# Strassen feed-forward stages rebuilt: units in sequence, the first product passed on in PSUM, row pairs for both halves, a fixed order on three engines

## The chip, the core and the metric

The kernel runs on one core of a Trainium2 chip. The metric is the device time of one execution in microseconds (us). The engines of the core are TensorE (PE: matmuls, and PEld: their weight loads), VectorE (DVE), ScalarE (ACT), GpSimd (POOL, here mostly an issuer of DMAs) and SyncE (SP, which issues the other DMAs). Each engine executes its own list of instructions in order and waits for semaphores of the others. [...]

## What is computed

One layer of a decoder trunk for 512 prompt tokens and 32 sample tokens (T = 544 together), width 1024:

```python
def swiglu(x, wg, wu, wd):
    return (jax.nn.silu(x @ wg) * (x @ wu)) @ wd

x = layer_norm(ALPHA * x + 0.5 * swiglu(x, ffn1_wg, ffn1_wu, ffn1_wd), ln1_g, ln1_b)
mix = ...            # RWKV-7 heads and a short convolution, both from x @ w_in, then @ w_out
x = layer_norm(ALPHA * x + mix, ln2_g, ln2_b)
x = layer_norm(ALPHA * x + 0.5 * swiglu(x, ffn2_wg, ffn2_wu, ffn2_wd), ln3_g, ln3_b)
```

The two feed-forward stages (1024 to 2816 to 1024) hold most of the matmuls. The change touches only them.

## The kernel before

**Layout.** Activations lie transposed: features on the 128 partitions, tokens along the row. A product in float32 precision is made of three matmuls: each operand is split into a high half (ScalarE, a copy that rounds to `F32R`) and a low half (VectorE, the operand minus its high half); the matmuls are high x high, high x low, low x high. So each weight tile costs one ScalarE and one VectorE pass beside its DMA. `hl` is a split weight tile, `hlb` a half-size one, `raw` the loaded one; `xhl` are the split inputs, `hhl` the split hidden rows, `z` the output sums.

**Strassen.** Both feed-forward products are done by a seven-product Strassen scheme (Winograd's form) on 2 x 2 blocks: tokens in two halves of 272 (`TB`), the inner dimension in two halves, the output rows in two. The 22 hidden row tiles come in chunks of 4, 4, 4, 4 and 6 (`CHUNKS`). Chunk 0's hidden rows are made by plain matmuls (`up`), the others by `pairs`. After each of chunks 0 to 3 `downs` multiplies its hidden rows by the down weights; chunk 4 goes to plain matmuls (`down`, `down_wide`).

- `pairs` works in units `u`: one unit makes gate or up of two hidden row tiles, so two units (even: gate, ended by Silu; odd: up, ended by a multiplication) make a row pair. A unit has seven products of 12 matmuls each, named by the weight tile: "a" twice, "x" twice, "y" twice, "b" once. `b1`, `b3`, `b4` are its PSUM banks (`mm` and `sm` in the profile, three and five of them). Bank `b1` goes on accumulating through a, y, x and b, and is copied out (to `cpb`) after each.
- `downs` has two groups of 14 products of 6 matmuls. Their inputs are seven combinations of the four hidden row tiles: `B11, B21, B22, NT1, NT2, T3, T4`.
- The weight combinations: "a" is a raw tile as loaded, "b" a half of the other raw tile, "x" that tile after an accumulating DMA by GpSimd has added the block A11 to it, "y" that tile after two VectorE additions. "y" and "a" free the raw tiles for the next loads (`feed`, `load`, five of them).

**What sets the order.** The program is recorded in the order of the generators, and a scheduler then places the instructions of every engine; it may pull a matmul of a later product ahead. Weight work is recorded by `plan`: an event for each part (`b`, `a`, `x`, `y`) at a lead, in products, ahead of the unit or group that needs it (`LEAD`, `LEAD_B`); `put` (L503) records the high and the low half together. Around them `held` keeps weight work behind the evictions of the product just recorded. Units are interleaved: in `pairs` (L562) the last two products of a unit (`tail`, L577) are recorded after the first two of the next.

**Hidden rows.** `put_h` (L366) makes the seven combinations. The halves of the inner dimension of the downs are row tiles (0, 1) and (2, 3) of a chunk: the first row pair is one half, the second pair the other. `NT2`, `T3` and `T4` mix both halves, so they wait for the second pair (the lines L383, L384, L387); `put_b22` splits both rows of `B22` at once.

**Names of lines used below.** L135/L136: high and low half of a weight tile. L143/L144: high and low half of other operands. L155 to L157: plain products. L521/L522: the additions for "y". L529/L535: the accumulating DMAs. L556 to L558: the three matmuls of a Strassen product. L599, L619, L627: VectorE's additions of a bank to `cpb` in a unit; L617, L623, L626: ScalarE's copies of `b1` in a unit. L646, L676: VectorE's additions in the downs; L662, L665: ScalarE's copies there.

Of the kernel before, what the change touches and what calls it, by code (L numbers as in the profile page):

```python
# [12 lines left out]
F32 = mybir.dt.float32  # L13
# [28 lines left out]
LEAD = dict(b=18, a=9, x=7, y=5)  # L42
LEAD_B = {0: 25, 1: 23}
# [18 lines left out]
def body(ctx: ExitStack, tc: tile.TileContext, xT, gu1, wd1, win, wo_c, wo_0, wo_1, gu2, wd2, wl, ln3, eye, lora, vec, cst,  # L62
# [260 lines left out]
    class Ffn:  # L323
        def __init__(self, z, gu, wd, ph, nf, late=1):
            self.z, self.gu, self.wd, self.na, self.nf, self.late = z, gu, wd, NA, nf, late
            self.ph, self.st, self.tst, self.w, self.nu = ph, ExitStack(), ExitStack(), {}, 0
            self.s1 = [cpb[:, 288 * h:288 * h + 288] for h in range(2)]
            self.lnr = cpb[:, 576:864]
# [37 lines left out]
        def put_h(self, j, r, parts):  # L366

            hb, (hk, sv) = self.hb, (x[:, r] for x in self.rows)
            lo, hi = slice(0, TB), slice(TB, T)

            def put(v, src):
                split(hb[:, v, 0, r], hb[:, v, 1, r], src)

            for part in parts:
                if j == 0 and part == "lo":
                    put(B11, hk[:, lo])
                elif j == 0:
                    DVE.tensor_tensor(hk[:, lo], hk[:, lo], hk[:, hi], op=OP.subtract)
                    put(NT1, hk[:, lo])
                elif part == "lo":  # L380
                    put(B21, sv[:, lo])
                elif part == "hi":
                    DVE.scalar_tensor_tensor(hk[:, lo], hk[:, lo], -1.0, sv[:, hi], op0=OP.mult, op1=OP.subtract)  # L383
                    DVE.tensor_tensor(hk[:, hi], sv[:, hi], hk[:, hi], op=OP.subtract)  # L384
                    put(slice(NT2, T3 + 1), hk.rearrange("p (v t) -> p v t", v=2))
                else:
                    DVE.scalar_tensor_tensor(sv[:, lo], hk[:, lo], -1.0, sv[:, lo], op0=OP.mult, op1=OP.subtract)  # L387
                    put(T4, sv[:, lo])

        def put_b22(self):  # L390
            split(self.hb[:, B22, 0], self.hb[:, B22, 1], self.rows[1][:, :, TB:])

        def up(self, m, h):
# [15 lines left out]
            if h:  # L409
                self.done.add(m)  # L410
                for m in [x for x in range(self.na) if x in self.done and (x < 2 or x - 2 in self.done)]:
                    if m not in self.made:
                        self.made.add(m)
# [1365 lines left out]
```

## Time and profile before

| | us |
|---|---|
| median of three runs | 1072.73 (1071.32 to 1073.76) |
| profiled execution, first to last instruction | 1069.3 |
| first feed-forward stage, Strassen part | 53.75 to 333.6 |
| second feed-forward stage, Strassen part | 742.6 to 1023.7 |
| one full chunk (4 units and the downs), repeated | 64.83 |

The profile is of one execution. Its page gives each engine's busy time and share of the span, then digits for 40 slices of the span, the DMA queues, the chain of work that ended last, and the costliest groups of instructions: line, engine, operation, output<-inputs, shape, xcount, then busy us, mean ns of one, and the idle time of the engine just before them with what ended it. A timeline row is start us, duration us, engine, line, operation, output<-inputs, shapes, count. A windows row gives busy time and count of instructions for PE, PEld, DVE, ACT and POOL in a stretch, then TensorE's granted clock, the DMA share and GB/s. Matmuls are pipelined, and the end of a row of TensorE is modelled.

### The profile page before, as it was taken

To read this page: it belongs to the slowest core of one execution; us is meant where nothing else is said; L and a number is where in the kernel's file an instruction comes from. 1 tells how busy PE (TensorE), PEld (TensorE's weight loads), DVE (VectorE), ACT (ScalarE), POOL (GpSimd) and SP (SyncE) were. 2 spreads that over 40 slices of the span, in tenths; PEclk is the share of its full clock that TensorE was granted. 3 is DMA by queue.
4 is the path that set the end of the run, shared out by engine and by line. 5 is a ranking of instruction groups with operands and counts; after the bars stand their busy time and mean duration, and the time that the engine had idled before them with its cause. 6 is when DMAs were issued, how large, how long until landed. Compare 5 with 4: busy or idle time off the path is not lost.

```text
span 1069.3 us, 22615 instructions
## 1 busy us (share of the span) xinstructions
PE 1050.8 (98%) x9178; PEld 1010.5 (95%) x9178; DVE 844.6 (79%) x1557; ACT 582.9 (55%) x1070; POOL 155.3 (15%) x273
## 2 busy tenths in 40 slices
PE   9999999999999999999999999999999999999997
PEld 8999999999999999899889988999999999999996
DVE  6797888979875777794578658888979888797657
ACT  5746465555553668654344435767555555655524
POOL 0121121211200032133101200001211212111000
PEclk9999999999999999999999999999999999999999
DMA  8558585676754223324145624334766948568512
GB/s 296 128 116 186 124 191 137 149 169 136 183 118 158 79 92 105 85 82 99 41 143 163 172 81 149 132 119 79 156 162 137 199 103 197 141 136 189 147 43 84
DMA packets 91528, 144.48 MB, mean 135 GB/s; under 512 B 34848, under 2 KB 52384, under 8 KB 91296
## 3 DMA queue, kind: packets, MB, share of 16 engines
q1 hardware_dynamic: 68144, 110.76, 33.7%
q0 software_dynamic: 22848, 31.72, 19.4%
q8 instruction: 72, 1.18, 0.4%
q10 hardware_dynamic: 432, 0.56, 0.2%
q14 instruction: 32, 0.26, 0.1%
HBM read 128.81 MB, written 9.75 MB: 130 GB/s over the span
## 4 chain that ended last, share of the span: by engine, by line
PE 77%; DVE 13%; ACT 6%; issue 2%; DMA 1%; POOL 0%; ACTq 0%; DVEq 0%; SPq 0%
PE mm L556 9%; PE mm L557 9%; PE mm L558 9%; PE mm L155 6%; PE sm L556 6%; PE sm L557 6%; PE sm L558 6%; PE mm L156 6%; PE mm L157 6%; DVE hhl L144 2%; DVE hl L136 2%; PE sm L444 1%; PE sm L1169 1%; ACT hl L135 1%; PE mm L787 1%
## 5 line engine op out<-in xcount | busy, mean ns | idle before, releaser
L136 DVE TENSOR_TENSOR hl<-raw,hl 128x1024 fp32r<-128x1024 f32 (+3 forms) x230 | 269.8, 1177 | 61.4 <-ACT hl L135 60.2
L135 ACT ACTIVATE hl<-raw 128x1024 fp32r<-128x1024 f32 (+3 forms) x230 | 232.8, 1020 | 67.3 <-DVE raw L522 43.5
L155 PE MATMUL mm<-xhl,hl 128*128 128x256 f32 (+1 forms) x704 | 208.9, 298 | 0.5 <-ACT xhl L143 0.5
L156 PE MATMUL mm<-xhl,hl 128*128 128x256 f32 (+1 forms) x704 | 203.0, 289 | 0.4 <-DVE xhl L144 0.4
L157 PE MATMUL mm<-xhl,hl 128*128 128x256 f32 (+1 forms) x704 | 202.0, 287 | 0.0
L155 PEld LDWEIGHTS mm<-xhl,hl 128*128 128x128 f32 x704 | 132.0, 188 | 6.7 <-issue 1.8
L156 PEld LDWEIGHTS mm<-xhl,hl 128*128 128x128 f32 x704 | 132.3, 188 | 2.4 <-DVE xhl L144 0.8
L157 PEld LDWEIGHTS mm<-xhl,hl 128*128 128x128 f32 x704 | 132.3, 188 | 0.3 <-issue 0.2
L558 PE MATMUL sm<-xhl,hl 128*128 128x272 f32 x432 | 125.2, 290 | 0.0
L557 PE MATMUL sm<-xhl,hl 128*128 128x272 f32 x432 | 124.4, 288 | 0.0
L556 PE MATMUL sm<-xhl,hl 128*128 128x272 f32 x432 | 124.1, 287 | 0.0
L556 PE MATMUL mm<-tv,hl 128*128 128x272 f32 x288 | 83.4, 290 | 0.3
L558 PE MATMUL mm<-tv,hl 128*128 128x272 f32 x288 | 83.4, 290 | 0.0
L557 PE MATMUL mm<-tv,hl 128*128 128x272 f32 x288 | 83.0, 288 | 0.0
L556 PEld LDWEIGHTS sm<-xhl,hl 128*128 128x128 f32 x432 | 81.3, 188 | 0.0
L557 PEld LDWEIGHTS sm<-xhl,hl 128*128 128x128 f32 x432 | 81.3, 188 | 0.0
L558 PEld LDWEIGHTS sm<-xhl,hl 128*128 128x128 f32 x432 | 81.3, 188 | 0.0
L535 POOL DMA_DIRECT2D raw<-in_wd x32 | 39.2, 1462 | 287.8 <-DVE hlb L144 225.2
L529 POOL DMA_DIRECT2D raw<-in_gu x36 | 43.3, 1203 | 203.0 <-DVE hlb L144 137.6
L557 PE MATMUL mm<-hhl,hl 128*128 128x272 f32 x192 | 56.0, 291 | 0.8 <-DVE hhl L144 0.2
L556 PE MATMUL mm<-hhl,hl 128*128 128x272 f32 x192 | 56.3, 299 | 0.3
L556 PEld LDWEIGHTS mm<-tv,hl 128*128 128x128 f32 x288 | 54.2, 188 | 1.9 <-ACT cpb L623 1.9
(421 smaller groups left out, 2713.5 us busy)
## 6 DMA issues: line engine op xcount, KB each, us to landing
raw<-in_gu SPq DMA_DIRECT2D x84, 512.0 KB, 4.4
raw<-in_gu POOLq DMA_DIRECT2D x36, 512.0 KB, 7.0
raw<-in_wd SPq DMA_DIRECT2D x32, 512.0 KB, 4.5
raw<-in_win SPq DMA_DIRECT2D x26, 512.0 KB, 3.6
raw<-in_wd POOLq DMA_DIRECT2D x32, 256.0 KB, 5.7
z<-sv POOLq DMA_DIRECT2D x16, 272.0 KB, 8.2
raw<-in_wo_c SPq DMA_DIRECT2D x8, 512.0 KB, 3.6
raw<-in_wd SPq DMA_DIRECT2D x8, 384.0 KB, 3.1
```

The source lines that it names most:

```text
L135: seen["hi"] = ACT.activation(hl[:, 0, a:b], raw[:, a:b], AF.Copy)
L136: seen["lo"] = DVE.tensor_tensor(hl[:, 1, a:b], raw[:, a:b], hl[:, 0, a:b].bitcast(F32), op=OP.subtract)
L144: return DVE.tensor_tensor(lo, x, hi.bitcast(F32), op=OP.subtract)
L155: PE.matmul(out, wh, src[:, 0, k, c0:c1], start=(start and i == 0), stop=False)
L156: PE.matmul(out, wh, src[:, 1, k, c0:c1], start=False, stop=False)
L157: seen["fill"] = PE.matmul(out, wl, src[:, 0, k, c0:c1], start=False, stop=(stop and i == n - 1))
L444: PE.matmul(o[i][h][:, :c1 - c0], block(hl, v, k), xhl[:, y, k, c0:c1], start=(k == 0 and j == 0), stop=(k == KD - 1 and j == 2), skip_gro ...
L529: POOL.dma_start(x.rearrange("p (s c) -> p s c", s=2), bass.AP(tensor=a11.tensor, offset=a11.offset, ap=[[2 * D, P], [P * 2 * D, 2], [1, 5 ...
L535: POOL.dma_start(four(x)[:, i], bass.AP(tensor=a11.tensor, offset=a11.offset, ap=[[DFF, P], [P * DFF, 2], [1, 256]]), accum_op=OP.add)
L556: PE.matmul(out, wh, src(0, i), start=(first and i == 0), stop=False, skip_group_check=True)
L557: PE.matmul(out, wh, src(1, i), start=False, stop=False, skip_group_check=True)
L558: PE.matmul(out, wl, src(0, i), start=False, stop=(i == n - 1), skip_group_check=True)
```

## The change

- *Units in sequence.* `pairs` runs the seven products of a unit one after the other, as a, x, y, y, x, a, b.
- *First product passed on in PSUM.* After the first "a" product ScalarE copies bank `b1` into bank `b4`, and the second "a" product goes on accumulating there. Before, `b4` began empty and VectorE added it to the copy of the first. The downs do the same with their first and last product on `b4` (`m1`, `m2`).
- *Row pairs feed both halves.* The host reorders the rows of the down weights, so that a row pair has one row in each half of the inner dimension. `put_h` makes all seven combinations of a pair when the pair is done; `B22` is split pair by pair.
- *Order of the downs.* Written as a list of names (`ORDER`, `FIRST`).
- *A fixed order on three engines.* Weight work (`PARTS`) and row work (`ROWS`) have places in half products, with places of their own for the high and the low half. `link` ties each ScalarE and each VectorE instruction of these stages to the one recorded before it, and `prod` does so for TensorE's products. Silu and multiplications of the even and odd units are done by halves of 272. `held` and `feed` go.

```diff
-LEAD = dict(b=18, a=9, x=7, y=5)
-LEAD_B = {0: 25, 1: 23}
+PARTS = {
+    "u0": dict(b=(-62, 7), a=(-31, 11), x=(-26, 7), c=(-17,), y=(-13, 3)),
...
+    "u3": dict(b=(-36, 10), a=(-12, 3), x=(-18, 11), c=(-6,), y=(-5, 1)),
...
+ROWS = {
+    (0, B11, 0): -17, (0, B11, 1): 1, (0, B21, 0): -3, (0, B21, 1): 13, (0, B22, 0): -25,
...
+LATE = -51
+ORDER = "m1 m1 m5 m5 u2 u2 m3 m3 u3 u3 m2 m2 u4 u4", "m1 m5 m1 m5 u2 u2 m3 m3 u3 u3 m2 m2 u4 u4"
+FIRST = "m1 m1 m5 m5 m2 u2 u2 m3 u3 m3 u3 m2 u4 u4", ORDER[1]
...
+        def link(self, q, e):
+            if self.fixed:
+                if self.prev[q] is not None:
+                    after(e, self.prev[q])
+                self.prev[q] = e
+            return e
...
+        def at(self, pos, f, *args):
+            self.ns += 1
+            heapq.heappush(self.steps, (pos, self.ns, f, args))
+
+        def run(self, pos):
+            while self.steps and self.steps[0][0] <= pos:
+                _, _, f, args = heapq.heappop(self.steps)
+                f(*args)
...
+        def put_h(self, p, *parts):
+
+            hk, sv = (self.rows[p][:, i] for i in range(2))
             lo, hi = slice(0, TB), slice(TB, T)
+            mix, n1 = cpb[:, 4 * TB:], cpb[:, 2 * TB:3 * TB]
+            ops = {NT1: (self.tt, n1, hk[:, lo], hk[:, hi]), T3: (self.tt, mix[:, hi], sv[:, hi], hk[:, hi]),
+                   NT2: (self.neg, mix[:, lo], hk[:, lo], mix[:, hi]), T4: (self.neg, hk[:, lo], mix[:, lo], sv[:, lo])}
...
+            now = 2 * self.t - 2
+            for part in parts:
+                if part in ops:
+                    f, *args = ops[part]
+                    self.at(now + ROWS[p, part, 2], f, *args, OP.subtract)
+            for part in parts:
+                if part in src:
+                    v = slice(NT2, T3 + 1) if part == NT2 else part
+                    dst = [self.hb[:, v, i, p] for i in range(2)]
+                    self.at(now + ROWS[p, part, 0], self.act, dst[0], src[part], AF.Copy)
+                    self.at(now + ROWS[p, part, 1], self.low, dst[1], src[part], dst[0])
...
+                    for part, pos in PARTS[kind].items():
+                        self.at(2 * t + pos[0], self.put, key, part)
+                        if part != "c":
+                            self.at(2 * t + pos[0] + pos[1], self.put_low, key, part)
...
         def prod(self, out, key, part, off, src, first, n=HK):
-            self.feed()
-            self.t += 1
+            self.run(2 * self.t)
...
+                if i == 0 and self.pe is not None:
+                    after(e, self.pe)
...
+            for u in range(m1 - m0):
                 j, i = divmod(u, 2)
-                s = self.rows[min(j, 1)]
+                a = 2 * TB * i
+                cp, s = cpb[:, a:a + 2 * TB], self.rows[j % 2]
+                b1, b4 = big()[:, :TB], sm()[:, :TB]
+                yield from prod(b1, u, "a", 0, xb(0, 0), True)
+                self.act(b4, b1, AF.Copy)
+                while self.add:
+                    self.tt(*self.add.popleft(), OP.add)
+                b3 = sm()[:, :TB]
+                yield from prod(b3, u, "x", HK, xb(0, TB), True)
+                self.act(cp[:, TB:], b3, AF.Copy)
+                yield from prod(b1, u, "y", HK, tb(0), False)
+                self.act(cp[:, 0:TB], b1, AF.Copy)
+                yield from prod(b3, u, "y", 0, xb(HK, TB), False)
+                self.tt(cp[:, 0:TB], cp[:, 0:TB], b3, OP.add)
...
+                yield from prod(b1, u, "x", 0, tb(1), False)
+                self.tt(cp[:, TB:], cp[:, TB:], b1, OP.add)
...
+                    if ci < LAST:
+                        self.put_h(j, B22)
+                yield from prod(b4, u, "a", HK, xb(HK, 0), False)
...
+                        self.put_h(j, B11, NT1, T3, NT2)
...
                 yield from prod(b1, u, "b", 0, tb(2), False)
...
+                        self.put_h(j, B21, T4)
...
+                def m1(q):
                     yield from prod(b1, q, "a", 0, B11, True)
-                    add(ds[q], b1[q])
+                    self.act(b4[q], b1[q], AF.Copy)
+
+                def m2(q):
+                    yield from prod(b4, q, "a", 1, B21, False)
+                    add(ds[q], b4[q])
+
+                def m5(q):
+                    yield from prod(b3, q, "x", 1, NT1, True)
+                    self.act(cp[q][:, 1], b3[q], AF.Copy, scale=-1.0)
+
+                def u2(q):
                     yield from prod(b1, q, "y", 1, NT2, False)
+                    self.act(cp[q][:, 0], b1[q], AF.Copy)
...
-        a["wd" + i] = tiles(g[f"ffn{i}_wd"][0]).reshape(KD, P, DFF)
+        order = list(first) + [b + k for b in (4, 8, 12) for k in (0, 2, 1, 3)] + list(range(16, MF))
+        a["wd" + i] = tiles(g[f"ffn{i}_wd"][0])[:, :, order].reshape(KD, P, DFF)
```

Of a place `(p, q)` in `PARTS`, p is where the high half of a part is recorded and q how much later the low half is, in half products from the start of the unit or group (a product of the downs is half as long as one of a unit); "c" are the additions for "y". In the downs `u3`, `m3` and `u4` follow the same pattern as `u2`: a product, then its eviction.

300 lines of the change are left out of this document (147 added, 153 removed).

## The prediction

> **What bounds the kernel now.** I read the page first: the shares of the engines and the chain that ended last, as shares by engine.
>
> ```profile
> span 1069.3 us, 22615 instructions
> PE 1050.8 (98%) x9178; PEld 1010.5 (95%) x9178; DVE 844.6 (79%) x1557; ACT 582.9 (55%) x1070; POOL 155.3 (15%) x273
> ...
> PEclk9999999999999999999999999999999999999999
> ...
> PE 77%; DVE 13%; ACT 6%; issue 2%; DMA 1%; POOL 0%; ACTq 0%; DVEq 0%; SPq 0%
> ```
>
> TensorE is the bound, at full clock, and the change removes no matmul: seven products for eight before and after. So it can only win the time in which TensorE's stream is held up, inside the two feed-forward stages. The sum is made as a difference against the profiled span of 1069.3 us; the median of the timed runs, 1072.73 us, is 3.4 us longer, which I leave as it is.
>
> How much is held up? A PE row lasts 0.29 us but the next starts 0.125 us later, so busy time hides short holds. I take starts instead. Next view: windows (us; busy time and count of instructions per engine).
>
> ```profile
> 146.20:179.50 33.30, 33.30 (x267) 33.30 (x267) 25.06 (x40) 19.58 (x34) 3.64 (x3) 1.00 0.70 166
> ...
> 112.00:176.80 64.80, 64.61 (x506) 63.54 (x505) 55.84 (x98) 35.73 (x62) 12.10 (x10) 1.00 0.69 155
> ...
> 53.75:111.95 58.20, 58.20 (x463) 57.80 (x462) 50.12 (x86) 31.18 (x54) 9.66 (x8) 1.00 0.65 146
> 306.40:333.50 27.10, 27.10 (x217) 27.00 (x216) 16.85 (x26) 15.38 (x27) 1.09 (x10) 1.00 0.45 130
> 742.70:801.95 59.25, 58.99 (x462) 58.00 (x461) 51.64 (x89) 32.60 (x57) 10.90 (x10) 1.00 0.69 152
> 996.30:1023.60 27.30, 27.30 (x217) 27.05 (x215) 17.64 (x27) 14.84 (x23) 0.00 (x0) 1.00 0.36 106
> ```
>
> The first row is an undisturbed stretch: 267 matmuls, one of them under way at its left edge, so 33.30 / 266 = 0.125 us from start to start. A full chunk repeats every 64.83 us, as the chain in order of time shows:
>
> ```profile
> 111.94 1.07 ACT hl L135
> ...
> 176.77 1.07 ACT hl L135
> ...
> 241.60 1.07 ACT hl L135
> ```
>
> It has 4 units x 7 products x 12 matmuls + 28 half-size products x 6 = 504 matmuls, or 504 x 0.125 = 63.1 us. So **1.7 us of each full chunk is hold-up**; there are three such chunks in each of the two stages: 10.2 us. The other four windows (first downs and part of chunk 1, and the last units, of each stage) give by count x 0.125, two of each count being under way at the edges: 0.6, 0.2, 1.75 and 0.4, together about 2.9. **About 13 us can be won at most**, 1.2%.
>
> [...]
>
> Where are the holds? Timeline, three places in chunk 1 (start us, us, engine, line; in brackets what the idle time waited for), then the chain that runs through the pairs-to-downs border.
>
> ```profile
> 114.59 0.40 ACT L626 ACTIVATE cpb<-mm 128x272 f32<-128x272 f32 x1 [0.76 <-PE mm L558]
> ...
> 115.04 0.19 PEld L556 LDWEIGHTS mm<-tv,hlb 128*128 128x128 f32 x1 [0.21 <-ACT cpb L626]
> 115.04 0.39 PE L556 MATMUL mm<-tv,hlb 128*128 128x272 f32 x1
> ...
> 115.27 0.29 PE L557 MATMUL mm<-tv,hlb 128*128 128x272 f32 x1
> ```
> ```profile
> 136.37 0.19 PEld L556 LDWEIGHTS mm<-hhl,hl 128*128 128x128 f32 x1 [0.25 <-ACT sv L662]
> ...
> 145.13 0.29 PE L558 MATMUL mm<-tv,hl 128*128 128x272 f32 x1
> ...
> 145.52 0.40 ACT L623 ACTIVATE cpb<-mm 128x272 f32<-128x272 f32 x1 [2.54 <-PE mm L558]
> ...
> 145.97 0.19 PEld L556 LDWEIGHTS mm<-tv,hl 128*128 128x128 f32 x1 [0.27 <-ACT cpb L623]
> ```
> ```profile
> 119.72 0.35 DVE z L646
> 120.06 0.35 DVE hhl L144
> 120.42 0.35 DVE hk L383
> 120.77 0.35 DVE hk L384
> 121.12 0.35 DVE sv L387
> 121.47 1.28 DVE hhl L144 x2
> 122.80 0.39 PE mm L557
> ```
>
> Two kinds. First, a bank that goes on accumulating must be copied out by ScalarE between two of its products (the first two fences); each such wait costs its own length plus about 0.1 us, since the first start after it is followed after 0.23 us (115.04 to 115.27) and not 0.125. Second, at the border the last row pair's sums and splits run one after the other on VectorE while the downs already need them.
>
> **The change part by part.**
>
> *Matmuls, weight loads, clock*: same number, same shapes: 0 us.
>
> *Border, pairs to downs.* With row pairs feeding both halves, the first pair's seven inputs can be made during units 2 and 3, and only the second pair's are left at the border. VectorE at the end of chunk 1, before (names: `hhl` the split inputs of the downs, `sv`/`hk` the rows, `z` the output):
>
> ```order
> L383 SCALAR_TENSOR_TENSOR hk<-hk,sv 128x272
> L384 TENSOR_TENSOR hk<-sv,hk 128x272
> L387 SCALAR_TENSOR_TENSOR sv<-hk,sv 128x272
> L144 TENSOR_TENSOR hhl<-sv,hhl 128x544
> L144 TENSOR_TENSOR hhl<-hk,hhl 128x2x272
> L144 TENSOR_TENSOR hhl<-sv,hhl 128x272
> L646 TENSOR_TENSOR z<-z,mm 128x272
> ```
>
> These stand after the first downs' additions; they are the chain above. The same engine and place now:
>
> ```order
> L400 TENSOR_TENSOR sv<-sv,sm 128x272
> L400 TENSOR_TENSOR cpb<-sv 128x272 x2
> L400 TENSOR_TENSOR hhl<-sv,hhl 128x272
> L403 SCALAR_TENSOR_TENSOR cpb<-sv,cpb 128x272
> L400 TENSOR_TENSOR hhl<-cpb,hhl 128x272
> L403 SCALAR_TENSOR_TENSOR sv<-mm,sv 128x272
> L403 SCALAR_TENSOR_TENSOR sv<-cpb,sv 128x272
> L400 TENSOR_TENSOR hhl<-sv,hhl 128x272
> L400 TENSOR_TENSOR hhl<-cpb,hhl 128x2x272
> L400 TENSOR_TENSOR hlb<-raw,hlb 128x512
> ```
>
> No addition to `z` and no first-pair work stands among them. I step them by 0.35 us for a 272-wide row (the chain's step) and 0.64 for a 544-wide one (1.28 for two). Zero is the end of the last unit's next-to-last product; the last product ends, and the downs begin, at 1.5. The first row starts at 0.1 and ends at 0.45, the two differences at 1.15, the low half of B11 at 1.5. The first downs need it for their second inner row, three matmuls and one in, at 1.5 + 0.5 = 2.0. NT1's low half ends at 2.2, needed at 3.5; NT2 and T3's at 3.9, needed at 5.0. All have half a microsecond or more, but for semaphores and the ScalarE half that stands ahead of each: a slip of a wait in B11 costs up to 0.2 us. I take 0.2 of the hold-up as staying here.
>
> *Evictions and the order of products.* In the downs the two copies are now four products apart ("u2 u2 m3 m3 u3 u3") where they were two, so the wait at 136.37 goes. In the units, every copy has exactly one other product (12 x 0.125 = 1.5 us) to hide under, four such windows in a unit (a to y and y to x on `b1`, x to y on `b3`, and x to b on `b1`, this one on VectorE). The 145.13 to 145.97 rows give the least a copy needs, from the last matmul's start to the next product's: 0.84 us. The window is 1.5 + 0.125 = 1.63, so **0.79 us of slack** for whatever ScalarE has in hand. The tightest place is after unit 1, where the first pair's splits now stand ahead of unit 2's first copy. ScalarE, before, at its first copy of unit 2 and what stands ahead:
>
> ```order
> L626 ACTIVATE cpb<-mm 128x272
> L135 ACTIVATE hl<-raw 128x1024
> L617 ACTIVATE cpb<-mm 128x272
> L135 ACTIVATE hl<-raw 128x1024
> L143 ACTIVATE hhl<-hk 128x272 x2
> L623 ACTIVATE cpb<-mm 128x272
> ```
>
> and now (`sm<-mm` is the new copy into the second bank):
>
> ```order
> L397 ACTIVATE hhl<-hk 128x272
> L397 ACTIVATE hl<-raw 128x1024
> L397 ACTIVATE hhl<-cpb 128x272
> L397 ACTIVATE hhl<-hk 128x272
> L397 ACTIVATE hhl<-cpb 128x2x272
> L397 ACTIVATE hlb<-raw 128x512
> L397 ACTIVATE hhl<-hk 128x272
> L397 ACTIVATE sm<-mm 128x272
> ```
>
> ```profile
> 124.02 1.05 ACT L135 ACTIVATE hl<-raw 128x1024 fp32r<-128x1024 f32 x1
> 124.97 0.39 ACT L662 ACTIVATE cpb<-mm 128x272 f32<-128x272 f32 x1
> 125.30 0.40 ACT L665 ACTIVATE cpb<-mm 128x272 f32<-128x272 f32 x1
> ```
>
> Seven rows now stand where four stood. By these starts a 1024-wide row steps by 0.95 and a 272-wide by 0.33; in proportion 0.55 for 544 or 512. From the end of unit 1's next-to-last product: product of the rows on VectorE done at 0.6, then 0.33 + 0.95 + 2 x 0.33 + 0.55 + 0.55 + 0.33 = 3.4, so the copy runs from 4.0 to 4.4; unit 2's third product may start at 1.5 + 1.5 + 1.5 = 4.5. It fits by 0.1, and loses 0.2 to 0.5 if one row slips. I leave 0.2 us per chunk here.
>
> *Counts on the side engines.* Over both stages VectorE loses 36 first-sum additions (one a unit) and 32 in the downs, and gains 8 separate splits: 60 fewer.
>
> ```profile
> L646 DVE TENSOR_TENSOR z<-z,mm 128x272 f32<-128x272 f32 x24 | 9.8, 429 | 0.0
> ...
> L617 ACT ACTIVATE cpb<-mm 128x272 f32<-128x272 f32 x12 | 4.7, 391 | 1.2 <-PE mm L558 0.2
> ...
> raw<-in_gu POOLq DMA_DIRECT2D x36, 512.0 KB, 7.0
> ```
>
> 60 x 0.43 = 26 us less on VectorE, some 3 us of each chunk's 55.8. ScalarE gains 58 rows x 0.39 = 23 us, on 35.7 of 64.8 busy. Both are hidden under TensorE as long as each keeps its place; without that cover the 3 us that VectorE loses in a chunk and the 3 that ScalarE gains nearly cancel. Sixty-eight of ScalarE's copies go from bank to bank, which no row shows; the nearest row is 0.39 us to SBUF. Bounds: nothing, and the 0.66 of a row twice as wide (0.55 by steps); even that lies inside the 0.79. I take 0.39.
>
> *DMA.* SyncE's list keeps its order and sizes. The accumulating loads are still issued behind the low half of "b"; what changes is where in ScalarE's fixed list the load's reader stands. Worst case: unit 3, whose "b" low half is placed eight half products (6.0 us) ahead of its "x" row, against 7.0 us to landing. VectorE's list reaches that low half early, though, directly after unit 1's sums (some 2 us before its place), so I count 0; if it did not, 1.0 us a chunk.
>
> **Sum.** Six chunks: 1.7 - 0.2 - 0.2 = 1.3 each, 7.8 us. Of the 2.9 at the ends I take half, since the first downs still depend on rows just made: 1.4. Together 9.2 us: span 1060.1, time **1063.5 us**.
>
> **The rivals.**
> - *All of it goes*: no new hold at all, 1072.7 - 13 = 1059.7. For it: every window above fits on paper. Against: two fit by 0.1 or by 0.5 less semaphores.
> - *A load takes the place of the copy*: ScalarE stands in order at an accumulating load, 1.0 us a chunk, and the copies behind it wait: 9.2 - 6 = 3.2, so 1069.5. For it: 6.0 against 7.0 us. Against: VectorE's lead.
> - *Late evictions, slower*: in each unit a copy finds ScalarE or VectorE just started on a 1024-wide row, 1.05 us against 0.79: 0.26 late plus 0.1. With 36 units and one such miss in each that is 13 us, all that can be won (**no change**, 1072.7); with 1.5 misses a unit 19.5 us, so 1072.7 + 6.5 = 1079. The point from which it decides is one miss per unit out of four windows. For it: before, the scheduler let other units' matmuls fill such a hold, the fixed order does not. Against: in the rows above no 1024-wide row stands where a copy is due except the one counted. [...]
>
> **How the numbers follow.** Forecast as worked out (0.1 to 0.8 us left per chunk, some 1061 to 1066): 0.55. All of it: 0.17. The load's wait: 0.11. Late evictions at about one per unit: 0.08; at more: 0.09. The range reaches from all of it, 1059.5, to past the load's wait, 1071. A measurement of this kernel tells about 0.2% (2 us) from no change: faster 0.83, same 0.08, slower 0.09.
>
> **What would show it.** Windows of a full chunk at about 63.5 us with 504 matmuls; no wait of TensorE on ScalarE's copies in the downs; VectorE near 53 us a chunk and ScalarE near 38; the chain that ended last no longer through VectorE at the border. It is wrong if a chunk stays at 64.8 or longer; then the waits before weight loads name the engine: ScalarE's `sm<-mm` and `cpb` rows (late evictions), or ScalarE itself waiting for `raw` (the load). It is also wrong if the stages' edges, which I cut only by half, grow.

## The result, and the profile after

| | before | after |
|---|---|---|
| median, us | 1072.35 (1071.32 to 1073.76, 4 runs) | 1058.99 (1058.69 to 1059.41, 4 runs) |
| ratio to before | | 0.9877, interval 0.9863 to 0.9891 |
| span of the profiled execution | 1069.3 | 1056.9 |
| first stage, 2184 Strassen matmuls, first to last start | 279.91 | 273.29 |
| second stage | 281.09 | 273.68 |

The change is 13.4 us faster, 12.4 by the spans. The forecast of 1063.5 was 4.5 us too slow, and the time lies 0.5 us outside the range. The bound, the engine and the sign were right; what was wrong is how much of the hold-up I left standing. What came is the first rival, "all of it goes".

The page of the kernel after: span, busy times, and the chain that ended last by engine.

```profile
span 1056.9 us, 22631 instructions
...
PE 1040.0 (98%) x9178; PEld 1007.2 (95%) x9178; DVE 829.7 (78%) x1497; ACT 592.9 (56%) x1128; POOL 155.6 (15%) x273
...
PE 86%; DVE 7%; ACT 4%; issue 1%; DMA 1%; POOL 0%; ACTq 0%; DVEq 0%; SPq 0%
```

TensorE's part of the chain went from 77% to 86%; VectorE's fell from 13% to 7%. Now the windows of the first downs of each stage, of two full chunks, and of the one chunk that is longer than the rest.

```profile
54.17:75.19 21.02, 21.02 (x170) 20.95 (x169) 19.23 (x35) 13.86 (x26) 3.30 (x4) 1.00 0.48 117
75.19:138.21 63.02, 63.02 (x506) 63.02 (x505) 54.38 (x91) 37.39 (x69) 12.11 (x12) 1.00 0.69 160
...
737.33:758.35 21.02, 21.02 (x170) 20.95 (x169) 19.88 (x36) 14.43 (x26) 4.21 (x5) 1.00 0.64 152
758.35:821.37 63.02, 63.02 (x506) 63.02 (x505) 54.45 (x91) 37.23 (x68) 12.08 (x11) 1.00 0.71 159
884.41:947.76 63.35, 63.31 (x506) 63.09 (x505) 54.42 (x91) 37.43 (x68) 11.80 (x11) 1.00 0.70 159
```

In a full chunk weight loads are busy for all of the 63.02 us, and 504 x 0.125 is 63.0: nothing is left of the hold-up. TensorE's starts, listed one by one, give the same (they are not shown here; sums of them below are called "by starts"). Adding them up (first matmul of a piece to the first of the next) gives where the time came from:

| us, both stages together | before | after | won |
|---|---|---|---|
| first downs, 2 x 168 matmuls | 43.75 | 42.04 | 1.7 |
| six full chunks, 6 x 504 | 388.67 | 378.51 | 10.2 |
| last six units, 2 x 504 | 128.58 | 126.42 | 2.2 |
| outside the stages (before, between, behind) | | | -1.7 |

The stages won 14.0 us; 1.7 were given back outside: 0.4 ahead of the first stage, 0.9 between the two, 0.4 behind the second. About half of that is only moved: in the kernel before, nine plain matmuls of the work behind a stage run while its last units are held up (at 329.98 to 330.46 and at 1020.07 to 1020.47), in the kernel after two. The seven others are 0.9 us, which count as won in the last units and as given back behind them. So the stages won about 13.1 us, 3.0 of it at their ends, and the rest of the kernel took 0.8 longer. The stretch between the stages, which no run touches, lasted 409.0 us before and 409.9 after, and 409.0 and 410.4 in two variants of the kernel before; what makes it vary was not looked for.

The two places that I had called tight, timeline of chunk 1 (start, duration, engine, line). First ScalarE's copy of unit 2 into the second bank, and the product that waits for it:

```profile
97.92 0.41 ACT L397 ACTIVATE hhl<-hk 128x272 fp32r<-128x272 f32 x1
98.24 0.37 ACT L397 ACTIVATE sm<-mm 128x272 f32<-128x272 f32 x1
...
99.13 0.29 PE L619 MATMUL sm<-xhl,hl 128*128 128x272 f32 x1
99.25 0.29 PE L615 MATMUL mm<-tv,hl 128*128 128x272 f32 x1
```

The copy ends at 98.61 and the product is due at 99.25: 0.64 us to spare, not 0.1. Second the border, where the low half of the last pair's B11 is made on VectorE:

```profile
117.06 0.44 DVE L400 TENSOR_TENSOR hhl<-sv,hhl 128x272 fp32r<-128x272 f32 x1
...
117.68 0.29 PE L615 MATMUL mm<-hhl,hl 128*128 128x272 f32 x1
117.81 0.29 PE L618 MATMUL mm<-hhl,hl 128*128 128x272 f32 x1
```

It ends at 117.50; the first matmul that reads it, high weights times low rows (L618), is due at 117.81: 0.3 us to spare and no hold. The one hold left in the six chunks, 0.3 us in the longest window above, begins at a load:

```profile
931.75 0.63 ACT L397 ACTIVATE hlb<-raw 128x512 fp32r<-128x512 f32 x1 [0.91 <-DMA raw<-in_gu]
932.29 0.66 ACT L397 ACTIVATE hk<-mm 128x272 f32<-128x272 f32 x2
...
932.39 0.29 PE L619 MATMUL sm<-hhl,hl 128*128 128x272 f32 x1
932.72 0.39 PE L615 MATMUL mm<-hhl,hl 128*128 128x272 f32 x1
```

ScalarE stands 0.91 us at the load, the copies behind it are late, and TensorE starts after 0.33 us instead of 0.125. It is not the accumulating load of the rival: `hlb` is the split of "b", which reads the raw tile as SyncE loaded it (L558). That load was issued at 924.38 and landed at 931.73, 7.3 us, where the median of its kind is 4.9.

### The profile page after: what moved, and what is told of

Same layout as the page of the kernel before. It is cut to its first block, busy times and chain, and to the rows that moved or that the text cites. A ratio compares the mean times of both kernels' runs of the same rounds, so it can differ in the third digit from the quotient of the medians.

```text
span 1056.9 us, 22631 instructions
## 1 busy us (share of the span) xinstructions
PE 1040.0 (98%) x9178; PEld 1007.2 (95%) x9178; DVE 829.7 (78%) x1497; ACT 592.9 (56%) x1128; POOL 155.6 (15%) x273
## 4 chain that ended last, share of the span: by engine, by line
PE 86%; DVE 7%; ACT 4%; issue 1%; DMA 1%; POOL 0%; ACTq 0%; DVEq 0%; SPq 0%
PE mm L619 10%; PE mm L615 10%; PE mm L618 10%; PE sm L619 7%; PE sm L615 7%; PE sm L618 7%; PE mm L176 7%; PE mm L177 7%; PE mm L178 7%; PE sm L503 1%; DVE hl L157 1%; PE sm L1246 1%; PE mm L864 1%; PE sm L828 1%; PE mm L503 1%
## 5 line engine op out<-in xcount | busy, mean ns | idle before, releaser
L400 DVE TENSOR_TENSOR hl<-raw,hl 128x1024 fp32r<-128x1024 f32 x156 | 187.8, 1222 | 21.6 <-ACT hl L397 20.1
L397 ACT ACTIVATE hl<-raw 128x1024 fp32r<-128x1024 f32 x156 | 162.3, 1054 | 58.6 <-DVE raw L400 53.9
L618 PE MATMUL sm<-xhl,hl 128*128 128x272 f32 x432 | 124.4, 288 | 0.0
L157 DVE TENSOR_TENSOR hl<-raw,hl 128x1024 fp32r<-128x1024 f32 (+3 forms) x74 | 79.3, 1084 | 13.2 <-ACT hl L156 12.9
L618 PE MATMUL mm<-tv,hl 128*128 128x272 f32 x288 | 83.1, 289 | 0.0
L618 PEld LDWEIGHTS sm<-xhl,hl 128*128 128x128 f32 x432 | 81.4, 188 | 0.0
L156 ACT ACTIVATE hl<-raw 128x1024 fp32r<-128x1024 f32 (+3 forms) x74 | 68.9, 945 | 19.8 <-DMA raw<-in_win 3.7
L606 POOL DMA_DIRECT2D raw<-in_gu x36 | 47.0, 1305 | 203.8 <-DVE hlb L400 128.1
L400 DVE TENSOR_TENSOR raw<-raw 128x512 f32<-128x512 f32 x104 | 71.8, 690 | 2.3
```

Source lines behind the costliest of these rows:

```text
L156: seen["hi"] = ACT.activation(hl[:, 0, a:b], raw[:, a:b], AF.Copy)
L157: seen["lo"] = DVE.tensor_tensor(hl[:, 1, a:b], raw[:, a:b], hl[:, 0, a:b].bitcast(F32), op=OP.subtract)
L397: return self.link(0, ACT.activation(*args, **kw))
L400: return self.link(1, DVE.tensor_tensor(out, a, b, op=op))
L606: POOL.dma_start(dst.rearrange("p (s c) -> p s c", s=2), bass.AP(tensor=a11.tensor, offset=a11.offset, ap=[[row, P], [P * row, 2], [1, 512 ...
L618: PE.matmul(out, wh, src(1, i), start=False, stop=False, skip_group_check=True)
```

## The experiments

Fourteen kernels. Each comparison had its own runs of the kernel before, whose medians lay between 1071.65 and 1071.85 us. Rows with base "after" go against its 1058.99 us from the comparison above; the medians of the kernel before differ by up to 0.7 us between comparisons, so a difference of medians below 1 us says nothing. "Stages" is the sum of both stages by starts in the one profiled execution, 546.97 us in the kernel after and 561.00 before; the profiled execution need not be the median one (it took 1100.43 us in e1_free and 1065.51 in f6_low3).

| run | base | median, us | against its base | stages, against its base |
|---|---|---|---|---|
| e1_free | after | 1107.69 | +48.7 | +41.4 |
| g3_act_free | after | 1165.32 | +106.3 | +105.7 |
| g4_dve_free | after | 1079.99 | +21.0 | +21.7 |
| g1_pe_free | after | 1067.10 | +8.1 | +7.2 |
| e7_border | after | 1089.77 | +30.8 | +30.3 |
| f3_nopass | after | 1073.95 | +15.0 | +15.1 |
| e2_near | after | 1067.03 | +8.0 | +7.7 |
| f4_copy2 | after | 1060.50 | +1.5 | +0.1 |
| f4_copy4 | after | 1063.99 | +5.0 | +5.2 |
| f6_low2 | after | 1060.33 | +1.3 | +1.8 |
| f6_low3 | after | 1063.50 | +4.5 | +4.6 |
| f9_first | after | 1058.99 | 0.0 | -0.2 |
| e8_before_far | before | 1073.65 | +1.9 | +2.6 |
| h1_before_pass | before | 1069.08 | -2.6 | -3.3 |

### How much slack the two tight places have

**The copy of unit 2, made twice and four times.**

```diff
-                self.act(b4, b1, AF.Copy)
+                for _ in range(2 if u == 2 and ci < LAST else 1): self.act(b4, b1, AF.Copy)
```

> The changed kernel with unit 2's first copy (bank to bank, on ScalarE) made twice in the six full chunks; the second y product of that unit waits for the later one, 0.37 us later. Theory (the copy has 0.64 us of slack, as the trace after shows): still in time, no hold, within 0.5 us of the changed kernel. Rival (0.1 us of slack, as my prediction's sum had it): 0.27 late plus 0.1 for the restart, 6 x 0.37 = 2.2 us slower.

> The same copy made four times, 3 x 0.28 to 3 x 0.37 = 0.85 to 1.1 us later. Theory (0.64 us of slack): 0.2 to 0.47 late plus 0.1, 6 x 0.3 to 6 x 0.57 = 1.8 to 3.4 us slower than the changed kernel. Rival (0.1 us of slack): 0.75 to 1.0 late plus 0.1, 5.1 to 6.6 us slower.

Twice: the chunks last 63.02 to 63.06 us as without it (but for the one with the load, 63.35 as without it). No hold. The median, 1.5 us above, lies between the two theories; the profiled execution, at 1059.35 us the fastest of four (up to 1061.25), has 0.1 of its excess in the stages, and where the slower ones lost theirs is not known. Four times, timeline of chunk 1:

```profile
98.64 1.62 ACT L397 ACTIVATE sm<-mm 128x272 f32<-128x272 f32 x4
...
99.44 0.28 PE L619 MATMUL sm<-xhl,hl 128*128 128x272 f32 x1
...
100.31 0.39 PE L615 MATMUL mm<-tv,hl 128*128 128x272 f32 x1 [0.58 <-ACT sm L397]
```

By its time alone this run speaks for the rival: 5.0 us, 5.2 by the stages, where the rival had 5.1 to 6.6. But the copies had a size that neither theory had: four that write the same tile take 1.62 us, so the last ends 1.25 later, not 0.85 to 1.1. In the chunk shown the next product starts 0.87 us after the matmul ahead of it, and in one other 0.92; there the first of the four copies itself begins 0.09 and 0.14 us later than in the kernel after. In the four chunks in which it begins at the same place the product starts after 0.78 us, 0.65 late: 1.25 - 0.65 is **0.60 us of slack**. With 0.1 of slack the hold would have been 1.15, and the doubled copy could not have been free.

**The low half of B11, made twice and three times.**

```diff
-                    self.at(now + ROWS[p, part, 1], self.low, dst[1], src[part], dst[0])
+                    for _ in range(2 if p == 1 and part == B11 else 1): self.at(now + ROWS[p, part, 1], self.low, dst[1], src[part], dst[0])
```

> The changed kernel with the low half of the second pair's B11, the last row the downs wait for at the border, made twice on VectorE in the six full chunks; it ends one 272-wide row, 0.35 us, later. Theory (0.3 us of slack there, as the trace after shows): 0.05 to 0.15 late plus up to 0.1, 0.3 to 1.5 us slower in all. Rival (0.2 us of hold is there already, as my prediction allowed): each of the 0.35 us counts, 2.1 us or more.

> The same low half made three times, 0.70 us later. Theory (0.3 us of slack): 0.4 late plus 0.1, 6 x 0.5 = 3.0 us slower than the changed kernel. Rival (no slack, a hold is there already): 6 x 0.70 = 4.2 us or more. Second rival (the downs could go on from the first row and hide it, 1 us or more of slack): no change.

Timeline of the border, with three of them:

```profile
117.30 1.39 DVE L400 TENSOR_TENSOR hhl<-sv,hhl 128x272 fp32r<-128x272 f32 x3
...
117.92 0.29 PE L615 MATMUL mm<-hhl,hl 128*128 128x272 f32 x1
...
118.74 0.39 PE L618 MATMUL mm<-hhl,hl 128*128 128x272 f32 x1 [0.53 <-DVE hhl L400]
```

Three take 1.39 us where one takes 0.44, so a repeated row costs 0.48 and not 0.35. TensorE starts 0.82 us after the matmul ahead (118.74 - 117.92), 0.70 late, for a row that is 0.95 late: 0.25 of slack. With two, one row of 0.48 makes TensorE 0.21 late, since 0.34 us pass there between two starts: 0.27 of slack. Both runs give the same **0.26 us**, and each adds about 0.1 for the matmul behind the wait. By the times alone they do not decide: 1.8 by the stages lies between the two sizes, and 4.6 lies in the rival's "4.2 us or more", because a repeated row is dearer than both theories had it. Against "a hold is there already" speaks that two rows cost 0.35 us a chunk (63.38 against 63.03) and not 0.48, three rows 0.82 and not 0.95, and that in the kernel after the matmul in question starts 0.13 us behind the one ahead of it (117.68 to 117.81).

### What keeps the order

**The links taken away on all three engines, and then on each engine alone.**

```diff
             if self.fixed:
-                if self.prev[q] is not None:
-                    after(e, self.prev[q])
                 self.prev[q] = e
...
-                if i == 0 and self.pe is not None:
-                    after(e, self.pe)
```

Here q is 0 for ScalarE and 1 for VectorE; the last two lines are TensorE's.

> The changed kernel with the links of the fixed order taken away on ScalarE, VectorE and TensorE: the program's text, tiles and sums are the same, but the scheduler orders the three engines again. Theory (the fixed order is what keeps each copy and each split in its place): the scheduler mixes products of different units and of downs, rows land later than their products want them, and the kernel is slower by 2 us or more, up to the 13 us of the change. Rival (the gain comes from the new parts alone, the row pairs and the first product passed on in PSUM, and the order only fixes what the scheduler would find): within 1 us of the changed kernel, 1058 to 1060.

> The changed kernel with the links on ScalarE alone taken away. Theory (ScalarE is the engine whose place counts: it stands in order at an accumulating load, 54 us of such waits when all three engines were free, and the copies behind it wait): most of the 48.7 us comes back here, over 24 us slower. Rival (VectorE's order or TensorE's made the loss): within 5 us of the changed kernel.

> The changed kernel with the links on VectorE alone taken away. Theory (the rows at the border have 0.26 us of slack, so a single 1024-wide split or addition put ahead of them there costs 0.1 to 1.0 us a chunk): 1 to 8 us slower. Rival (VectorE's late sums hold up ScalarE and with it the loads): over 24 us. Third (VectorE's order would come out the same): no change.

> The changed kernel with the link between TensorE's products alone taken away; ScalarE and VectorE keep their order. Freed on all three engines it lost 48.7 us. Theory (the loss comes from ScalarE and VectorE, whose rows fall behind wide weight splits and late loads): TensorE alone freed costs little, within 5 us of the changed kernel. Rival (the scheduler's mixing of products makes the loss): half of it or more, over 24 us.

Without the order the change is not a gain but a loss, far beyond the 2 to 13 us expected: 48.7 us against the kernel after, 1.033 of the time before (1.032 to 1.035). ScalarE is the engine that counts: alone freed it loses 106.3, VectorE 21.0, TensorE 8.1. The parts don't add up: with all three free the loss is less than with ScalarE alone. An engine that is free beside two that are not is placed against their lists; that this is the reason is not shown. A part of the loss is TensorE's clock (last section): the mean granted clock of the profiled execution was 0.972 with ScalarE freed, 0.994 with VectorE, 0.992 with all three and 0.998 with TensorE, where the kernel after has 0.999. What is missing to 1, times the span, is by my estimate the most that it can have cost: 33, 6, 9 and 2 us, against 1 in the kernel after. The view of waits (waiting instruction, releaser, us in total, times, longest), ScalarE freed:

```profile
ACT hl L397 <- DMA raw<-in_wd: 59.5, 12, 7.9
ACT hlb L397 <- DMA raw<-in_gu: 56.9, 19, 4.9
PEld mm L615 <- ACT hhl L397: 38.1, 6, 8.0
ACT hl L397 <- DMA raw<-in_gu: 37.7, 20, 3.3
```

ScalarE stands 154 us at these loads, and the rows of the downs (`hhl`) come up to 8 us late behind it. By who issued them, 87.5 us are at GpSimd's accumulating loads and 66.5 at SyncE's plain ones. In the kernel after the same three waits come to 0.9 + 2.7 + 0.3 us. The 54 us that my expectation took from the run with all three freed were all at SyncE's plain loads, not at accumulating ones as it says. VectorE freed:

```profile
ACT hl L397 <- DMA raw<-in_wd: 18.9, 7, 4.2
...
PEld mm L615 <- ACT sm L397: 13.7, 12, 3.3
```

Again ScalarE stands at a load, and the copies to the second bank (`sm`) are late behind it; the sizes I expected (a split put ahead of a border row) were too small because of that. TensorE freed, its longest waits are on additions in the downs, half a microsecond each:

```profile
PEld mm L615 <- DVE z L400: 4.1, 8, 0.5
```

Both expectations for TensorE missed, the nearer one by 3 us.

### The border

**The first pair's rows put back to the border.**

```diff
+            late = lambda part: p == 0 and part not in (B11, NT1)
+            edge = 2 * self.pair_end + 28 + 1
...
-                    self.at(now + ROWS[p, part, 2], f, *args, OP.subtract)
+                    self.at(edge if late(part) else now + ROWS[p, part, 2], f, *args, OP.subtract)
```

The high and low halves get the same `edge`; `pair_end` is the product at which unit 1's last "x" product ends, and 28 half products are the two units behind it, so `edge` is the same place in the last unit.

> The changed kernel with the first row pair's T3, NT2, T4, B21 and B22 rows and splits put back to the border between units and downs, where the kernel before made them; nothing else moves. Theory (the burst on VectorE at the border was the largest hold of the kernel before, 0.75 us of the 1.6 in a full chunk): at least 0.75 us in each of six full chunks comes back, 4.5 us, and by the lengths of the rows on VectorE up to 2.4 us a chunk, 14.6 us, so 1063.5 to 1073.5. Rival (units and order did it, the border has slack for the burst): under 2 us slower.

It cost 30.8 us, twice the largest size expected: 68.0 us a chunk, 5.0 more. Windows at the border of chunk 1 (us, then PE, PEld, DVE, ACT, POOL busy with counts, TensorE's granted clock, DMA share, GB/s):

```profile
115.00:118.00 3.00, 3.00 (x26) 3.00 (x25) 2.75 (x6) 0.14 (x1) 0.00 (x0) 1.00 1.00 201
118.20:121.40 3.20, 0.34 (x3) 0.12 (x1) 2.71 (x7) 1.81 (x5) 0.00 (x0) 1.00 1.02 260
121.40:124.70 3.30, 3.27 (x13) 2.97 (x14) 3.25 (x9) 2.60 (x6) 0.00 (x0) 0.51 0.00 0
124.80:128.00 3.20, 3.20 (x27) 3.20 (x26) 2.33 (x4) 2.66 (x7) 1.21 (x1) 0.99 0.06 5
```

TensorE is held for 3.05 us while VectorE makes seven rows. Then it works for 3.3 us at a granted clock of 0.51 and starts 13 matmuls where the window ahead has 26 in 3.0. So 3.05 is the burst. By the two windows behind the hold (0.51 over 3.30 us, 0.99 over 3.20, and the 0.1 between them) I estimate some 3.4 us at half clock, which costs 1.7, and the first two starts behind the hold, after 0.59 and 0.39 us instead of 0.227, make up most of the rest of the 5.0.

### The evictions

**The copies of the downs near again.**

```diff
-ORDER = "m1 m1 m5 m5 u2 u2 m3 m3 u3 u3 m2 m2 u4 u4", "m1 m5 m1 m5 u2 u2 m3 m3 u3 u3 m2 m2 u4 u4"
+ORDER = "m1 m1 m5 m5 u2 u2 u3 u3 m3 m3 m2 m2 u4 u4", "m1 m5 m1 m5 u2 u2 u3 u3 m3 m3 m2 m2 u4 u4"
```

`FIRST` likewise; the addition of `zh` follows m3.

> The changed kernel with the order of the downs u2 u2 u3 u3 m3 m3 instead of u2 u2 m3 m3 u3 u3: the copy of the u2 product has again only one other product of 0.75 us to hide under, as in the kernel before, and needs 0.84 us. Theory (the distance of the copies is what removed the hold at 136.37): the hold of about 0.30 us comes back once in each of the two groups of each of the eight downs, 16 x 0.30 = 4.8 us slower, some 1063.8. It may be less where the four-half m3 window now hides something else, but at least 8 x 0.30 = 2.4. Rival (the wait was the scheduler's doing and not the distance's): no change, within 1 us.

8.0 us, where 4.8 were expected; not 0.30 in every group but, in the full chunks of the first stage, 0.78 in the first group and 0.07 in the second, and in the second stage up to 1.9 in the first group. Timeline of chunk 1, then of a chunk of the second stage:

```profile
121.70 0.63 ACT L397 ACTIVATE hlb<-raw 128x512 fp32r<-128x512 f32 x1
...
121.87 0.29 PE L619 MATMUL mm<-hhl,hl 128*128 128x272 f32 x1
...
122.22 0.69 ACT L397 ACTIVATE hk<-mm 128x272 f32<-128x272 f32 x2
...
122.67 0.39 PE L615 MATMUL mm<-hhl,hl 128*128 128x272 f32 x1 [0.51 <-ACT hk L397]
...
873.92 0.63 ACT L397 ACTIVATE hlb<-raw 128x512 fp32r<-128x512 f32 x1 [0.98 <-DMA raw<-in_gu]
...
874.89 0.39 PE L615 MATMUL mm<-hhl,hl 128*128 128x272 f32 x1 [1.61 <-ACT hk L397]
```

The copy `hk<-mm` stands behind a weight split in ScalarE's list, and in the second stage that split stands at a load. With the copies four products apart, as in the kernel after, the same rows are covered. So the distance pays for what stands ahead of a copy as well as for the copy.

**The same distance in the kernel before**, in the second of the two groups, the one with the hold at 136.37 (the expectation calls it the first):

```diff
-                for q in range(2):
-                    yield from prod(b4, q, "a", 1, B21, True)
-                    add(ds[q], b4[q])
+                if g == 0:
+                    ...
                 for q in range(2):
                     yield from prod(b1, q, "y", 1, NT2, False)
                     hold(ACT.activation(cp[q][:, 0], b1[q], AF.Copy))
+                if g:
+                    ...
```

> The kernel before with one piece of the change alone: in the first of the two groups of each downs, the m2 products stand between the u2 products and the u3 products, so that the copy of u2 has two more products to hide under. Theory (each wait on a copy is removed by distance alone, without the fixed order): the hold of 0.30 us at 136.37 and its likes goes in each of the eight downs, 2.4 us faster than the kernel before, 1069.9. Rival (the scheduler fills or moves the holds anyway, so distance alone gives nothing): within 0.7 us of 1072.4, or slower as the scheduler's choices fall otherwise.

Slower by 1.9 us (ratio 1.0006 to 1.0023): the rival. The wait on the downs' copy, 2.0 us in eight, is gone from the view of waits, but others came: that on the units' copy rose from 1.9 to

```profile
PEld mm L556 <- ACT cpb L623: 3.0, 10, 0.5
```

and in each full chunk of the first stage five starts of 0.16 to 0.21 us and two of 0.23 appear where the hold was, for which that view names nobody. In this kernel distance alone wins nothing while the scheduler places the rest; the first group was not tried.

**The first product not passed on in the downs of the kernel after.**

```diff
-                    self.act(b4[q], b1[q], AF.Copy)
+                    add(ds[q], b1[q])
...
-                    yield from prod(b4, q, "a", 1, B21, False)
+                    yield from prod(b4, q, "a", 1, B21, True)
```

> The changed kernel with the first product no longer passed on in PSUM in the downs: VectorE adds it to the output by itself, and the second bank starts empty; the units keep the copy. ScalarE loses 32 rows of 0.37 us, VectorE gains 32 of 0.35 (two of them stand ahead of the low halves of B21 at each border). Theory (at the border VectorE has 0.26 us of slack for B11 and more for what comes after, and the copies to PSUM are not on the path): within 1 us of the changed kernel. Rival (VectorE is full at the border, so its two extra rows, 0.7 us, come up on TensorE): 6 x 0.44 to 6 x 0.8 = 2.6 to 4.8 us slower.

15.0 us: more than the whole change won, and three times the rival's most. Timeline, VectorE and TensorE in chunk 1:

```profile
121.50 0.43 DVE L400 TENSOR_TENSOR hhl<-hk,hhl 128x272 fp32r<-128x272 f32 x1
121.85 0.78 DVE L400 TENSOR_TENSOR z<-z,mm 128x272 f32<-128x272 f32 x2
...
122.33 0.40 PE L615 MATMUL mm<-hhl,hl 128*128 128x272 f32 x1 [1.02 <-DVE z L400]
...
132.70 2.35 DVE L400 TENSOR_TENSOR hl<-raw,hl 128x1024 fp32r<-128x1024 f32 x2
...
133.98 0.39 PE L619 MATMUL mm<-hhl,hl 128*128 128x272 f32 x1 [0.67 <-DVE hl L400]
```

My expectation counted the two additions as rows ahead of others. They are evictions: bank `b1` may not go on (u2) before VectorE has read it, and in VectorE's list they stand behind all rows of the border. That costs 1.3 us; behind them the weight splits are late, another 0.9. So 2.2 us a chunk.

**The same part alone in the kernel before.** The edit is the reverse one, in the downs.

> The kernel before with one piece of the change alone: in the downs, the first product goes on in PSUM (ScalarE copies it to the second bank, m2 adds to it there, VectorE adds once), the scheduler orders as before. VectorE loses 32 additions. Theory (passing on takes the first product's eviction off VectorE where VectorE is late; undone in the changed kernel it cost 15.0 us): the border's hold of 0.75 us shrinks by the two additions that stand in that chain, 0.35 to 0.7 us in each of eight downs, 2.8 to 5.6 us faster than the kernel before, 1066 to 1069. Rival (in the kernel before the border's hold hangs on the last row pair's rows and splits, with the additions behind them; the addition's place is the scheduler's to choose): within 1 us of the kernel before.

2.6 us faster than before (0.9967 to 0.9985), just under the 2.8 expected; not all for the expected reason. TensorE's waits in the kernel before, then in this one:

```profile
PEld mm L557 <- DVE hhl L144: 2.3, 7, 0.4
...
PEld mm L556 <- ACT sv L662: 2.0, 8, 0.3
PEld mm L556 <- ACT cpb L623: 1.9, 7, 0.3
```
```profile
PEld mm L556 <- ACT cpb L662: 1.6, 8, 0.2
...
PEld mm L556 <- ACT sv L662: 1.4, 8, 0.2
PEld mm L557 <- DVE hhl L144: 1.3, 6, 0.2
```

The border's wait (`hhl` L144) shrank by 1.0 us; the units' wait on L623, 1.9 us, went; a new one on L662 came. Passing on in PSUM, in the downs, wins by itself, a fifth of the change. Which of the other parts would win without the order was not tried one by one.

### The first downs

```diff
-FIRST = "m1 m1 m5 m5 m2 u2 u2 m3 u3 m3 u3 m2 u4 u4", ORDER[1]
+FIRST = ORDER
```

> The changed kernel with the first downs of each stage in the order of the other downs (u2 u2 m3 m3 u3 u3 m2 m2 in place of m2 u2 u2 m3 u3 m3 u3 m2). By starts, the first downs of the two stages took 21.50 and 22.25 us before and take 21.02 now. Theory (their own order is part of the 3.9 us won at the ends: the first downs' rows are made late and this order asks for them later): 0.3 to 1.2 us a stage come back, 0.6 to 2.4 us slower than the changed kernel. Rival (the ends were won by the copies and additions being off the path, not by that order): no change, first downs 21.0 us.

No change: 1058.99 us in both, and the first downs take 20.91 and 21.12 us. Their own order did not win the ends.

## Why the prediction was too slow, point by point

- **What bounds it.** Right. TensorE at full clock, hold-ups in the two stages, nothing else. The full chunks lost 10.2 of the 10.2 us that I had counted there. "About 13 us can be won at most" holds too: by starts the stages won 14.0, and 0.9 of that only moved behind them. At the ends the window counts gave 2.9 us, and 3.0 were won.
- **Weight loads as a measure.** In the full chunk before (112.00 to 176.80) weight loads are busy for 63.54 of the 64.80 us and matmuls for 64.61, so six chunks had 7.6 us to win by the one and 1.1 by the other; starts said 10.2, and 10.2 came. Weight loads were nearer than matmul busy time but too low. In the chunk after, loads are busy for all of 63.02 us, so there loads and starts agree.
- **The residuals: the step that failed.** "I take 0.2 of the hold-up as staying here" at the border and "I leave 0.2 us per chunk here" at unit 2's copy, 2.4 us in all, were put in for slips that didn't happen: 0.26 us and 0.60 us of slack are shown by the repeated rows. At the border the sum itself had 0.5 us in hand, about twice what is there, and the outcome did not hang on it. At the copy my sum was wrong as well: it started all of ScalarE's rows behind unit 1's multiplication, 0.6 us after the end of its next-to-last product. The first of them is the half of B22, which doesn't need that multiplication and starts 0.4 us earlier, at 94.92.
- **The ends: the other half of it.** "Of the 2.9 at the ends I take half": 3.0 came, 1.6 us more than the 1.4 taken. By the run on the first downs' order it was not that order. In the trace before, TensorE waits there at ScalarE's copies (L623, L626, L662), at one row of the border and at one weight split; in the trace after none of these waits is left. So it was the same two kinds of hold as in the full chunks; which part of the change removed each at the ends was not separated.
- **The time around the span.** The 3.4 us "which I leave as it is" are 2.1 in the kernel after (1058.99 - 1056.9): 1.3 us. A run's time is 1.7 to 2.1 us above its own span in the runs on record (1058.70 and 1056.9 in the kernel after), so by my estimate about 1.6 of the 3.4, against 0.3 of the 2.1, were only that the profiled execution was faster than the median; this part of the miss is chance. And the 0.8 us that the rest of the kernel took longer were not in the sum. Together: 2.4 + 1.6 - 0.8 + 1.3 = 4.5, the whole miss. That the time fell below the range is no more than that: with all hold-up gone the range ended at 1059.5, and medians of the kernel before lie between 1071.65 and 1072.73.
- **Evictions, distance.** Right in direction: near copies cost 8.0 us. Too small in size, because I priced the copy and not what stands ahead of it.
- **The fixed order.** I counted it as the form of the change, with the late evictions as its risk. The runs make it the condition of the gain. What giving up the interleaving of the units cost by itself is not shown by any run here. With TensorE's order freed products of different groups could have mixed again, and the kernel lost 8.1 us, but they hardly did: cut wherever the output or the operands change, the six full chunks have 270 pieces in that run, 264 in the kernel after and 306 before. Not taken back by themselves, in any run, are the units in sequence and the copy in the units; what each of them is worth stays open.
- **A load takes the place of the copy.** Not as I had it: at accumulating loads ScalarE waits 1.2 us in both stages together, so "I count 0" was right. The same hold at a plain load happens once in six chunks, 0.3 us, and was not among the rivals. That loads are the right thing to fear is shown by the runs without order, where ScalarE stands at loads of both kinds for up to 154 us.
- **Counts on the side engines.** Forecast near 53 and 38 us a chunk on VectorE and ScalarE; measured 54.4 and 37.4. Sixty rows fewer on VectorE (1557 to 1497), 58 more on ScalarE, as counted. The copy from bank to bank takes 0.38 us on average (68 of them); 0.39 was taken.

## What to carry to other kernels

Where every needed row is due at a known time and the sum says it arrives before that, the hold is zero and not a bit of itself: keep the doubt in the range, and measure a slack by making its last instruction twice. A bank that goes on accumulating should be read by the engine that has room at that place, and its read counts as a wait and not as a row. When a change moves work and fixes the order at once, ask what the scheduler would do with the work alone: here it would have turned 13 us of gain into 36 us of loss.

## What the hardware showed that I had not expected

A long hold could cost more than its length. Behind the 3.05 us hold at the border above, TensorE's granted clock was 0.51 for 3.3 us, and matmuls started every 0.227 us (ten steps from 122.41 to 124.68) instead of 0.125. A shorter hold was enough with ScalarE's order freed: TensorE was busy for 0.31 us of 2.10, and the 3.00 us behind ran at 0.52, with 14 matmuls. But the longer hold is not always the dearer one: with all three freed TensorE was busy for 0.28 us of 2.40, and the 3.00 us behind ran at 1.00, with 23. The windows of the two, ScalarE freed and then all three:

```profile
57.20:59.30 2.10, 0.31 (x3) 0.09 (x1) 2.07 (x7) 1.73 (x6) 0.00 (x0) 1.00 0.00 0
59.40:62.40 3.00, 3.00 (x14) 3.00 (x15) 2.41 (x4) 1.15 (x5) 0.00 (x0) 0.52 0.00 0
```
```profile
123.20:125.60 2.40, 0.28 (x3) 0.06 (x1) 0.72 (x3) 2.20 (x5) 0.00 (x0) 1.00 0.23 92
125.70:128.70 3.00, 3.00 (x23) 2.82 (x23) 3.00 (x8) 2.75 (x8) 0.00 (x0) 1.00 0.00 0
```

What made the difference between the two was not shown. In the border run the windows behind the hold have 0.51 in chunk 1 (121.40 to 124.70) and 0.54 in chunk 2 (189.40 to 192.90). With 1.7 us in each of the six chunks, by my estimate, the clock cost about 10 of the 30.8 us. The mean granted clock of that execution speaks for about the same: 0.989 over 1088.1 us is 12 us missing to full clock, against 1 in the kernel after.

A row made again into the same tile was dearer here than one in a mixed list: three equal VectorE rows took 1.39 us and four equal ScalarE copies 1.62, 0.48 and 0.42 us for each further one, where the steps between different rows of the same width were 0.35 and 0.32. Whether the shared tile makes it so, or that each of these rows waits for the one ahead, was not tried.
